# First loads reordered, the last softmax inverses spread by TensorE, and the last attention group written in separate steps

## The chip, the cores and the metric

The kernel runs on one core of a Trainium2 chip. The metric is the device time of one execution in microseconds (us). The engines are TensorE (PE, matrix products into PSUM), VectorE (DVE), ScalarE (ACT), GpSimd (POOL) and SyncE (SP, which only issues transfers here). Each works through its own instructions in order. Transfers (DMA) are issued from the queues of SP, ACT and POOL.

## The reference

One decoder block over 512 positions of width 1024 with two attention branches of 8 heads of 64 each, both fed by one input projection. Cut to what matters:

```python
h = rms_norm(x, norm_g)
fq, fk, fv, fz, mq, mk, mv, mz, ga, gb, fl = split_cols(h @ w_in, ...)
# FoX: causal softmax(q k^T / 8 + c_i - c_j), c the running sum of log_sigmoid(fl + b_f)
y_fox = fox_attention(norm(fq), norm(fk), fv, log_f) * silu(fz)
# MoBA: rope on q and k; own block causal, other blocks of 256 by top-k (all of them at this length)
y_moba = moba_attention(rope(norm(mq)), rope(norm(mk)), mv) * silu(mz)
merged = sigmoid(ga + b0) * (y_fox @ w_fox) + sigmoid(gb + b1) * (y_moba @ w_moba)
out = x + merged @ w_out
```

All is float32.

## The kernel before

**Products.** Each float32 operand is split into a high and a low part in the type float32r (`...h` and `...l`: the high one is a cast, mostly by ACT, the low one a subtraction by DVE). A product is three PE matmuls: high by high, high by low and low by high. `Zh`, `Zl` are the parts of the scaled input (one block of 128 channels by 512 positions for each `xt` of 256 KB), `wh_...`, `wl_...` those of the weights, which come in as `wr_...`.

**Start.** Eight matmuls on zeros (`warm_ps`, L82) precede the real ones. The constants `cs` (128x68, 35 KB, with the norm gains that `Zh` is scaled by) are loaded by the ACT queue. Then `load_g` loads a block xt and splits it, and `load_quarters` loads the first weights `wr_fqa` in pieces: the first k block by the ACT queue behind `cs`, the second by the SP queue behind xt0, each with a DVE cast of 128x256 of its own, and then two blocks at a time. Calls of both alternate, so the SP queue carries xt0, w1, xt1, xt2, w2:4, xt3, xt4, w4:6, xt5, xt6, w6:8, xt7. PE's first products (L358 to L360, `fqa`) use them.

**Attention.** Four groups of four heads follow: FoX a, FoX b, MoBA a, MoBA b. The functions of a group are `Tr(pr)` (transposes of the normed q and k of a pair of heads, L494 and L496, their scaling into `QS`, `KH`, and a transfer by the ACT queue that copies `KH` to the other 64 partitions, L507), `Aa(h)` (logits `lg` by L530 and L531, row maximum and mask by DVE, exponential by ACT with the row sum), `Bb(h)` (transposes of the probabilities, L576, into `p_a`, `p_b`, `p_cc`; their split into `pth` and `ptl`, L582 and L583; the products with v into `pv`, L586 and L587; the sum of both halves into `ypair` with the help of the copy `ysh`) and `Yp(pr)` (product with the inverse row sums and with silu(z), L626 and L627, and the split into `yh` and `yl`, called `yhm`, `ylm` in the MoBA branch).

**The inverse row sums.** `inverse_sums` takes the reciprocals, a 128x8 block with one column for a head and query tile. `sums_out` transposes it (`p_ri`, L555), copies it by ACT (`rinv_t`, L557) and stores it to DRAM; `sums_in` loads it back by two broadcast transfers of the ACT queue (L566) into `rinv_bc`, 64 partitions for each head. `Yp` multiplies by it.

**What stands between.** While a group is worked through, `inter` mixes its steps evenly with units of other products: the projections of the next group, and in the last group two units of `mzb` (`pz`) and six of `wf0` to `wf2` (`pf`, the FoX branch times its output weights, 12 matmuls of 128x512 a unit, L644 to L646). `wf3` follows the last group on its own.

**Gates.** Then come the gate projections `GA0`, `GA1`, `GB0`, `GB1`. Each is a Winograd scheme of seven products (`A11`, `S3`, `A12`, `S2`, `S1`, `A22`, `S4`; L715 to L718 into `pb_GA`), whose left sides are `Gh`, `Gl` or the sums `S0` to `S3`, which POOL's queue loads from DRAM (L258, eight loads). ACT copies some products out of PSUM (`e_GA`, L725) and splits the weights (`wh_GA`, L110); DVE makes `wl_GA` (L112). `Yp(1)` of the last group is emitted behind the third unit of `GA0`. Then come `wm0` to `wm3`, which use `yhm`, and the output products `wo0` to `wo3`.

**Order.** The program is written in this order; a scheduler then orders the instructions of each engine by its own simulated times, so an instruction can come earlier or later than it is written. All three change spots are subject to it.

Of the kernel before, what the change touches and what calls it, by code (L numbers as in the profile page):

```python
# [13 lines left out]
P = 128  # L14
# [15 lines left out]
def fox_moba_kernel(ctx: ExitStack, tc, xT, x, w_in, w_fl, w_fox, w_moba, w_out, cst, rope, out):  # L30
# [31 lines left out]

    cs = con.tile([P, C_END], F32, name="cs")
    rp = con.tile([P, NT, 32], F32, name="rp")
    wfl = con.tile([P, KT, 8], F32, name="wfl")
    nc.scalar.dma_start(out=cs, in_=cst)

# [6 lines left out]
    mask = con.tile([P, 512], F32, name="mask")  # L74
    wsc = t2("u", 4, "wsc", (P, 2))
# [18 lines left out]
    XT, Z = {}, {}  # L94

    def load_g(*ks):
        for k in ks:
            xt = XT[k] = t2("y", 15, f"xt{k}")
            nc.sync.dma_start(out=xt, in_=xT[:, k, :])
# [24 lines left out]
    def load_quarters(name, c0, hf, between):  # L124
        raw = sb.tile([P, 4, CW], F32, name=f"wr_{name}{hf}", tag="wr", bufs=WR)
        hi = sb.tile([P, 4, 264], F32R, name=f"wh_{name}{hf}", tag="wh", bufs=4)
        lo = sb.tile([P, 4, 264], F32R, name=f"wl_{name}{hf}", tag="wl", bufs=4)
        for q in range(2):
            first = hf == 0 and q == 0
            for k in (slice(0, 1), slice(1, 2)) if first else (slice(2 * q, 2 * q + 2),):  # L130
                (nc.scalar if first and k.start == 0 else nc.sync).dma_start(
                    out=raw[:, k], in_=w_in[c0 // CW, :, 4 * hf + k.start:4 * hf + k.stop, :])
                if first:
                    V.tensor_copy(hi[:, k, :CW], raw[:, k])
                else:
                    A.activation(hi[:, k, :CW], raw[:, k], AF.Copy)
                V.tensor_tensor(out=lo[:, k, :CW], in0=raw[:, k], in1=hi[:, k, :CW].bitcast(F32), op=OP.subtract)
            load_g(*between[q])
        chunks.setdefault(name, []).append((hi, lo))
# [343 lines left out]
    def attn_group(br, half, gq, gk):  # L483
# [76 lines left out]
        def sums_in(pr):  # L560
            if last and pr:
                rb = st["r", pr] = t2("u", 4, "rinv_bc")
            else:
                rb = st["r", pr] = stage["pool"].tile([P, S], F32, name="rinv_bc", tag="rinv_bc", bufs=1)
# [4 lines left out]
        def Bb(h):  # L569
            def go():  # L570
                pts, vt = st[h], VT[f"{br}v{half}"]
                o = h % 2
                pv = pst("pv", 1, "pv")
# [39 lines left out]
                if o == 0:  # L613
                    sums_out(pr)
                elif pr:
                    sums_in(1)
# [391 lines left out]
```

## Time and profile before

| | |
|---|---|
| three runs | 444.06, 443.63, 441.45 us; median 443.63 |
| profiled execution | 444.28 us, of which the span of the profile is 442.5 |
| mean granted PE clock | 0.996 |
| busy: PE, DVE, ACT, POOL | 428.4, 314.7, 262.5, 87.6 us |
| share of the span | 97%, 71%, 59%, 20% |
| read from and written to HBM | 46.27 and 6.32 MB |

Times in the rows count from the start of the span. A row of the timeline gives start, duration, engine, line, operation, result and operands, and in brackets the idle time before it with what ended it. A row of the waits gives the total, the count and the longest. The chain is the work that ended last, followed backwards; PEclk is the granted PE clock in tenths. Matmuls overlap, so the time of one is longer than the distance between two.

### The profile page before, as it was taken

What the parts mean: (1) busy time and instruction counts of PE and PEld (TensorE: products, weight loads), DVE (VectorE), ACT (ScalarE), POOL (GpSimd) and SP (SyncE); (2) the same over time, 40 slices, a digit from 0 to 9 for tenths busy, and PEclk for the clock granted to TensorE, in tenths of its full rate; (3) what the DMA queues carried; (4) which work ended last, traced back from release to release, by engine and by line L of the source; (5) the groups of instructions that cost most, each with busy time, mean ns of one, the idle gap of its engine ahead of it and who ended that gap; (6) DMA issues with size and microseconds to landing.
All of it is one profiled execution on the core that took longest, in us unless ns stands there. A gap on an engine that the chain in (4) does not pass through costs nothing.

```text
span 442.5 us, 8082 instructions
## 1 busy us (share of the span) xinstructions
PE 428.4 (97%) x3100; PEld 403.9 (91%) x3100; DVE 314.7 (71%) x563; ACT 262.5 (59%) x491; POOL 87.6 (20%) x106
## 2 busy tenths in 40 slices
PE   6999999999999999999999999987999999999996
PEld 5998899999999998899998878877999989989996
DVE  5559994777998869676956689928978786584311
ACT  5676544876777769887765876717655545531100
POOL 1059200224142950134621002200000000000000
PEclk9999999999999999999999999998999999999999
DMA  8962164424377413303304212663134405624231
GB/s 261 388 246 69 54 205 137 111 74 136 110 233 209 103 55 120 119 13 122 106 14 132 95 24 90 232 203 96 60 133 126 160 1 183 197 96 152 88 96 48
DMA packets 25991, 56.40 MB, mean 127 GB/s; under 512 B 3296, under 2 KB 11936, under 8 KB 25952
## 3 DMA queue, kind: packets, MB, share of 16 engines
q1 hardware_dynamic: 14528, 39.95, 27.4%
q10 hardware_dynamic: 10272, 11.74, 9.0%
q0 software_dynamic: 1152, 4.19, 2.8%
q8 instruction: 24, 0.39, 0.4%
q14 instruction: 15, 0.12, 0.1%
HBM read 46.27 MB, written 6.32 MB: 119 GB/s over the span
## 4 chain that ended last, share of the span: by engine, by line
PE 85%; ACT 6%; DMA 4%; DVE 2%; issue 1%; ACTq 0%; SPq 0%; DVEq 0%
PE pb_GB L718 3%; PE pb_GB L717 3%; PE pb_GB L715 3%; PE po L815 3%; PE po L817 3%; PE po L816 3%; PE pb_GA L715 2%; PE pb_GA L717 2%; PE pb_GA L718 2%; PE pv L587 2%; PE pv L586 2%; PE lg L530 2%; PE lg L531 2%; PE pm L644 2%; PE pm L645 2%; PE pm L646 2%
## 5 line engine op out<-in xcount | busy, mean ns | idle before, releaser
L535 ACT ACTIVATE p<-p,negm 128x128 f32<-128x128 f32 (+1 forms) x64 | 35.7, 558 | 12.5 <-DVE negm L533 11.2
L310 POOL TENSOR_TENSOR ff<-ss,mh 128x8 f32<-128x8 f32 x16 | 27.1, 1699 | 79.6 <-DVE ss L308 77.3
L533 DVE CUSTOM_DVE_ANT_0 p<-lg,mask 128x128 f32<-128x128 f32 (+1 forms) x64 | 30.5, 485 | 5.8 <-PE lg L531 5.6
L815 PE MATMUL po<-wh_wo,mgh 128*128 128x256 f32 x96 | 27.1, 282 | 0.0
L817 PE MATMUL po<-wh_wo,mgl 128*128 128x256 f32 x96 | 27.0, 282 | 0.0
L816 PE MATMUL po<-wl_wo,mgh 128*128 128x256 f32 x96 | 26.9, 281 | 0.0
L825 DVE TENSOR_TENSOR ot<-po,xr 128x256 f32<-128x256 f32 x16 | 6.6, 424 | 24.7 <-PE po L817 23.6
L110 ACT ACTIVATE wh_wo<-wr_wo 128x1024 fp32r<-128x1024 f32 x8 | 8.5, 1061 | 21.6 <-PE po L817 8.0
L530 PE MATMUL lg<-KH,QS 128*128 128x128 f32 (+1 forms) x64 | 20.7, 332 | 0.4 <-DMA KH<-KH 0.4
L112 DVE TENSOR_TENSOR wl_GB<-wr_gb,wh_GB 128x1024 fp32r<-128x1024 f32 x14 | 16.8, 1223 | 4.2 <-ACT wh_GB L110 3.3
L110 ACT ACTIVATE wh_GB<-wr_gb 128x1024 fp32r<-128x1024 f32 x14 | 14.6, 1059 | 8.6 <-PE pm L645 2.5
L612 DVE TENSOR_TENSOR ypair<-pv,ysh 64x512 f32<-64x512 f32 x16 | 11.0, 688 | 10.8 <-ACT ysh L611 10.7
L816 PEld LDWEIGHTS po<-wl_wo,mgh 128*128 128x128 f32 x96 | 18.1, 189 | 0.0
L815 PEld LDWEIGHTS po<-wh_wo,mgh 128*128 128x128 f32 x96 | 18.1, 189 | 0.0
L817 PEld LDWEIGHTS po<-wh_wo,mgl 128*128 128x128 f32 x96 | 18.1, 188 | 0.0
L715 PE MATMUL pb_GA<-Gh,wh_GA 128*128 128x256 f32 x48 | 14.3, 298 | 3.3 <-ACT e_GA L725 3.3
L112 DVE TENSOR_TENSOR wl_GA<-wr_ga,wh_GA 128x1024 fp32r<-128x1024 f32 x14 | 16.6, 1219 | 1.2 <-ACT wh_GA L110 1.1
L110 ACT ACTIVATE wh_GA<-wr_ga 128x1024 fp32r<-128x1024 f32 x14 | 14.5, 1054 | 4.5 <-DVE wr_ga L679 2.7
L504 DVE SCALAR_TENSOR_TENSOR QS<-p_qT,cs,QS 64x512 fp32r<-64x512 f32 x16 | 12.0, 750 | 6.6 <-ACT QS L503 6.2
L611 ACT ACTIVATE ysh<-pv 64x512 f32<-64x512 f32 x16 | 9.5, 593 | 9.8 <-PE pv L587 8.0
L112 DVE TENSOR_TENSOR wl_wo<-wr_wo,wh_wo 128x1024 fp32r<-128x1024 f32 x8 | 9.8, 1222 | 7.4 <-ACT wh_wo L110 7.4
L583 DVE TENSOR_TENSOR ptl<-p_a,pth 128x512 fp32r<-128x512 f32 x16 | 11.0, 687 | 5.1 <-ACT pth L582 5.0
(448 smaller groups left out, 1798.8 us busy)
## 6 DMA issues: line engine op xcount, KB each, us to landing
wr_ga<-in_w_in_dram SPq DMA_DIRECT2D x8, 512.0 KB
wr_gb<-in_w_in_dram SPq DMA_DIRECT2D x8, 512.0 KB
wr_wo<-in_w_out_dram SPq DMA_DIRECT2D x8, 512.0 KB
xt<-in_xT_dram SPq DMA_DIRECT2D x8, 256.0 KB
x<-in_x_dram SPq DMA_DIRECT2D x8, 256.0 KB
s_dramh<-sum_sh ACTq DMA_DIRECT2D x8, 256.0 KB
s_draml<-sum_sl ACTq DMA_DIRECT2D x8, 256.0 KB
KH<-KH ACTq DMA_DIRECT2D x16, 128.0 KB
```

What stands on the lines that cost most here:

```text
L110: A.activation(hi[:, :, 0:n], src, AF.Copy)
L112: eng.tensor_tensor(out=lo[:, q, 0:n], in0=src[:, q], in1=hi[:, q, 0:n].bitcast(F32), op=OP.subtract)
L310: G.tensor_tensor(out=f2, in0=ss.rearrange("p t h -> p (t h)"), in1=mh, op=OP.pow)
L530: T.matmul(lg[:, :n], qs[:, qt], kh[:, :n], start=True, stop=False)
L533: V.tensor_tensor_reduce(pt, lg[:, :n], mask[:, 512 - n:512], -0.125, 3.0e38, op0=OP.add, op1=OP.min, accum_out=mkn[:, hh, i:i + 1])
L535: A.activation(pt, pt, AF.Exp, bias=mkn[:, hh, i:i + 1], scale=-1.0, accum_out=rs[:, hh, i:i + 1])
L715: T.matmul(o, hi[:, k, cc], lh, start=(n < 3 and c == 0 and k == 0), stop=False, skip_group_check=True)
L717: T.matmul(o, hi[:, k, cc], ll, start=False, stop=False, skip_group_check=True)
L718: T.matmul(o, lo[:, k, cc], lh, start=False, stop=(k == 3), skip_group_check=True)
L815: T.matmul(p[:, :CW], gh[:, st], hi[:, k, :CW], start=(kk == 0), stop=False)
L816: T.matmul(p[:, :CW], gh[:, st], lo[:, k, :CW], start=False, stop=False)
L817: T.matmul(p[:, :CW], gl[:, st], hi[:, k, :CW], start=False, stop=(kk == KT - 1))
```

## The change

Three parts, all in the order or the way of work; what is computed stays the same.

1. **First loads.** `first_loads` issues all x blocks and first weights before anything else: xt0 and then `cs` by the ACT queue; w0:2 (256 KB in one), xt1, w2:4, xt2, xt3, w4:8 (512 KB in one), xt4 to xt7 by the SP queue. `first_split` makes one DVE cast of 128x512 for w0:2.
2. **The last pair's inverse sums.** For the last pair of heads of the last group `sums_out` and `sums_in` go. In `Yp(1)` POOL spreads the inverses into `rinv_w` (two copies of 128x4x64, an inverse repeated 64 times for each head and tile), four PE transposes put them into a PSUM bank (`p_rinv`, in place of a bank of `lg`), and DVE multiplies silu(z) by that bank.
3. **The last group.** `Bb(h)` becomes `Bb(h, 0)` (transposes and split) and `Bb(h, 1)` (products with v) for the heads 2 and 3, and the units of `mzb`, `wf0` to `wf3` stand at places written out by hand: after the steps 0, 2 and 5 one, after step 3 two, and one after each step from `Aa(3)` on, so one stands between the transposes of a head and its products. `wf3` is thus no longer behind the group.

```diff
--- before.py
+++ after.py
@@ -60,11 +60,33 @@
         return pst("tp", 3, name)
 
 
+    XT, RAW = {}, {}
+
+    def first_loads():
+        def xt(eng, k):
+            XT[k] = t2("y", 15, f"xt{k}")
+            eng.dma_start(out=XT[k], in_=xT[:, k, :])
+
+        def w(k0, k1):
+            hf = k0 // 4
+            if hf not in RAW:
+                RAW[hf] = sb.tile([P, 4, CW], F32, name=f"wr_fqa{hf}", tag="wr", bufs=WR)
+            nc.sync.dma_start(out=RAW[hf][:, k0 - 4 * hf:k1 - 4 * hf], in_=w_in[0, :, k0:k1, :])
+        xt(nc.scalar, 0)
+        w(0, 2)
+        nc.scalar.dma_start(out=cs, in_=cst)
+        xt(nc.sync, 1)
+        w(2, 4)
+        xt(nc.sync, 2)
+        xt(nc.sync, 3)
+        w(4, 8)
+        for k in range(4, KT):
+            xt(nc.sync, k)
+
+
     cs = con.tile([P, C_END], F32, name="cs")
     rp = con.tile([P, NT, 32], F32, name="rp")
     wfl = con.tile([P, KT, 8], F32, name="wfl")
-    nc.scalar.dma_start(out=cs, in_=cst)
-
     def col(c, n=1):
         return cs[:, c:c + n]
 
@@ -72,6 +94,8 @@
     triU = con.tile([P, P], F32, name="triU")
     ones = con.tile([P, P], F32, name="ones")
     mask = con.tile([P, 512], F32, name="mask")
+    enter("start")
+    first_loads()
     wsc = t2("u", 4, "wsc", (P, 2))
     V.memset(wsc, 0.0)
     A.activation(wsc, wsc, AF.Square)
@@ -91,12 +115,11 @@
 
     Gh = con.tile([P, KT, S], F32R, name="Gh")
     Gl = con.tile([P, KT, S], F32R, name="Gl")
-    XT, Z = {}, {}
-
-    def load_g(*ks):
+    Z = {}
+
+    def split_x(*ks):
         for k in ks:
-            xt = XT[k] = t2("y", 15, f"xt{k}")
-            nc.sync.dma_start(out=xt, in_=xT[:, k, :])
+            xt = XT[k]
             zh, zl = Z[k] = [stage["pool"].tile([P, S], F32R, name=f"Z{hl}{k}") for hl in "hl"]
             A.activation(zh, xt, AF.Copy, scale=col(C_NG + k))
             V.scalar_tensor_tensor(zl, xt, col(C_NG + k), zh.bitcast(F32), op0=OP.mult, op1=OP.subtract)
@@ -121,22 +144,19 @@
         V.tensor_tensor(out=lo[:, :, CW:264], in0=f, in1=hi[:, :, CW:264].bitcast(F32), op=OP.subtract)
         chunks.setdefault(name, []).append((hi, lo))
 
-    def load_quarters(name, c0, hf, between):
-        raw = sb.tile([P, 4, CW], F32, name=f"wr_{name}{hf}", tag="wr", bufs=WR)
-        hi = sb.tile([P, 4, 264], F32R, name=f"wh_{name}{hf}", tag="wh", bufs=4)
-        lo = sb.tile([P, 4, 264], F32R, name=f"wl_{name}{hf}", tag="wl", bufs=4)
+    def first_split(hf, between):
+        raw = RAW[hf]
+        hi = sb.tile([P, 4, 264], F32R, name=f"wh_fqa{hf}", tag="wh", bufs=4)
+        lo = sb.tile([P, 4, 264], F32R, name=f"wl_fqa{hf}", tag="wl", bufs=4)
         for q in range(2):
-            first = hf == 0 and q == 0
-            for k in (slice(0, 1), slice(1, 2)) if first else (slice(2 * q, 2 * q + 2),):
-                (nc.scalar if first and k.start == 0 else nc.sync).dma_start(
-                    out=raw[:, k], in_=w_in[c0 // CW, :, 4 * hf + k.start:4 * hf + k.stop, :])
-                if first:
-                    V.tensor_copy(hi[:, k, :CW], raw[:, k])
-                else:
-                    A.activation(hi[:, k, :CW], raw[:, k], AF.Copy)
-                V.tensor_tensor(out=lo[:, k, :CW], in0=raw[:, k], in1=hi[:, k, :CW].bitcast(F32), op=OP.subtract)
-            load_g(*between[q])
-        chunks.setdefault(name, []).append((hi, lo))
+            k = slice(2 * q, 2 * q + 2)
+            if hf == 0 and q == 0:
+                V.tensor_copy(hi[:, k, :CW], raw[:, k])
+            else:
+                A.activation(hi[:, k, :CW], raw[:, k], AF.Copy)
+            V.tensor_tensor(out=lo[:, k, :CW], in0=raw[:, k], in1=hi[:, k, :CW].bitcast(F32), op=OP.subtract)
+            split_x(*between[q])
+        chunks.setdefault("fqa", []).append((hi, lo))
 
     COLS = {}
     off = 0
@@ -559,18 +579,15 @@
 
         def sums_in(pr):
             if last and pr:
-                rb = st["r", pr] = t2("u", 4, "rinv_bc")
-            else:
-                rb = st["r", pr] = stage["pool"].tile([P, S], F32, name="rinv_bc", tag="rinv_bc", bufs=1)
+                return
+            rb = st["r", pr] = stage["pool"].tile([P, S], F32, name="rinv_bc", tag="rinv_bc", bufs=1)
             for o in range(2):
                 A.dma_start(out=rb[o * HD:(o + 1) * HD, :],
                             in_=R_dram[hb + 2 * pr + o].rearrange("t p -> (t p)").partition_broadcast(HD))
 
-        def Bb(h):
-            def go():
-                pts, vt = st[h], VT[f"{br}v{half}"]
-                o = h % 2
-                pv = pst("pv", 1, "pv")
+        def Bb(h, part=None):
+            def turn():
+                pts = st[h]
 
                 def blk(dst, i, j):
                     T.transpose(dst, pts[i][:, j * P:(j + 1) * P], ident)
@@ -582,9 +599,6 @@
                     A.activation(hi[:, :n], p[:, :n], AF.Copy)
                     V.tensor_tensor(out=lo[:, :n], in0=p[:, :n], in1=hi[:, :n].bitcast(F32), op=OP.subtract)
                     return hi, lo
-                def pvm(j, hl, c0, n, start, stop):
-                    T.matmul(pv[:, P * j:P * j + n], vt[:, j, h, :], hl[0][:, c0:c0 + n], start=start, stop=False)
-                    T.matmul(pv[:, P * j:P * j + n], vt[:, j, h, :], hl[1][:, c0:c0 + n], start=False, stop=stop)
                 pa = tp("p_a")
                 for i in range(4):
                     blk(pa[:, i * P:(i + 1) * P], i, 0)
@@ -598,6 +612,21 @@
                 for i in range(2, 4):
                     blk(pc[:, (i - 2) * P:(i - 1) * P], i, 2)
                 hc = spl(pc, 256)
+                st["t", h] = ha, hbb, hc
+
+            def go():
+                if part != 1:
+                    turn()
+                if part == 0:
+                    return
+                vt = VT[f"{br}v{half}"]
+                o = h % 2
+                ha, hbb, hc = st["t", h]
+                pv = pst("pv", 1, "pv")
+
+                def pvm(j, hl, c0, n, start, stop):
+                    T.matmul(pv[:, P * j:P * j + n], vt[:, j, h, :], hl[0][:, c0:c0 + n], start=start, stop=False)
+                    T.matmul(pv[:, P * j:P * j + n], vt[:, j, h, :], hl[1][:, c0:c0 + n], start=False, stop=stop)
                 pvm(0, ha, 0, 512, True, False)
                 pvm(1, hbb, 0, 384, False, False)
                 pvm(3, hbb, 384, 128, False, False)
@@ -610,7 +639,7 @@
                 sh = t2("u", 4, "ysh")
                 A.activation(sh[me, :], pv[ot, :], AF.Copy)
                 V.tensor_tensor(out=y[me, :], in0=pv[me, :], in1=sh[me, :], op=OP.add)
-                if o == 0:
+                if o == 0 and not (last and pr):
                     sums_out(pr)
                 elif pr:
                     sums_in(1)
@@ -622,8 +651,19 @@
                 gp = 2 * (half == "b") + pr
                 yh = t2("y", 15, f"yh{br}{gp}", dt=F32R)
                 yl = t2("y", 15, f"yl{br}{gp}", dt=F32R)
-                zr = st["r", pr]
-                (V if (br, gp) == ("m", 3) else G).tensor_tensor(out=zr, in0=ZS[br, gp], in1=zr, op=OP.mult)
+                if last and pr:
+                    zr, rb = ZS[br, gp], pst("lg", 2, "p_rinv")
+                    h0 = hb + 2 * pr
+                    rw = t2("u", 4, "rinv_w")
+                    for o in range(2):
+                        G.tensor_copy(rw.rearrange("p (t o d) -> p t o d", o=2, d=HD)[:, :, o, :],
+                                      ri[:, h0 + o, :, None].to_broadcast([P, NT, HD]))
+                    for t in range(NT):
+                        T.transpose(rb[:, t * P:(t + 1) * P], rw[:, t * P:(t + 1) * P], ident)
+                    V.tensor_tensor(out=zr, in0=zr, in1=rb, op=OP.mult)
+                else:
+                    zr = st["r", pr]
+                    G.tensor_tensor(out=zr, in0=ZS[br, gp], in1=zr, op=OP.mult)
                 V.tensor_tensor(out=y, in0=y, in1=zr, op=OP.mult)
                 A.activation(yh, y, AF.Copy)
                 V.tensor_tensor(out=yl, in0=y, in1=yh.bitcast(F32), op=OP.subtract)
@@ -631,7 +671,7 @@
             return go
 
 
-        return ([Tr(0)], [Aa(0), Aa(1), Tr(1), Bb(0), Aa(2), Bb(1), Yp(0), Aa(3)], [Bb(2), Bb(3)], [Yp(1)])
+        return ([Tr(0)], [Aa(0), Aa(1), Tr(1), Bb(0), Aa(2), Bb(1), Yp(0), Aa(3)], [Bb(2), Bb(3)] if not last else [Bb(2, 0), Bb(2, 1), Bb(3, 0), Bb(3, 1)], [Yp(1)])
 
 
     FS, MG = {}, {}
@@ -871,10 +911,9 @@
         for u in filler(names):
             u()
 
-    enter("start")
-    load_g(0)
-    load_quarters("fqa", COLS["fqa"], 0, ((1, 2), (3, 4)))
-    load_quarters("fqa", COLS["fqa"], 1, ((5, 6), (7,)))
+    split_x(0)
+    first_split(0, ((1, 2), (3, 4)))
+    first_split(1, ((5, 6), (7,)))
     nc.sync.dma_start(out=wfl, in_=w_fl)
     load_fl("fka", COLS["fka"], 0)
     load_fl("fka", COLS["fka"], 1)
@@ -926,11 +965,19 @@
                     u()
                     store[0]()
                 fill[2 * k + 8], fill[2 * k + 8 + 1] = with_sums, with_store
-        inter(body + ([following] if n < 3 else []) + tail, fill)
+        if n < 3:
+            inter(body + [following] + tail, fill)
+        else:
+            fill += filler(["wf3"])
+
+            for k, u in enumerate(body + tail):
+                u()
+                for f in {0: (0,), 2: (1,), 3: (2, 3), 5: (4,)}.get(k, (k - 3,) if k > 7 else ()):
+                    fill[f]()
+
         if n < 3:
             body, tail = nxt[1][:1] + gate + nxt[1][1:], nxt[2]
             gate = nxt[3]
-    seq(["wf3"])
     enter("gates")
     load_sums()
     fill = filler(["GA0", "GA1", "GB0"])
```

## The prediction

> **What bounds the kernel now.** I read the page's busy times and its slices first, then PE's waits, then the chain that ended last around the longest wait, and last the timeline of the first 8 us.
>
> ```profile
> span 442.5 us, 8082 instructions
> PE 428.4 (97%) x3100; PEld 403.9 (91%) x3100; DVE 314.7 (71%) x563; ACT 262.5 (59%) x491; POOL 87.6 (20%) x106
> PE   6999999999999999999999999987999999999996
> PEclk9999999999999999999999999998999999999999
> ```
>
> TensorE (PE) is busy for 97% of the span, so apart from PE's own work only 442.5 - 428.4 = 14.1 us of idle time can be won, and whatever PE does at a low clock. The slices show where: the first, a soft spot at slices 27 to 28, and the end. The sum below is made against this execution's own time of 444.28 us (span 442.5, and 1.8 around it). The median of the three runs is 443.63, the lowest 441.45. PE's waits, as total, times and longest:
>
> ```profile
> PE pb_GA L715 <- ACT e_GA L725: 3.3, 1, 3.3
> PE fqa L358 <- DVE wh_fqa L134: 2.4, 1, 2.4
> PE pv L586 <- ACT pth L582: 1.3, 2, 0.7
> PE pv L587 <- DVE ptl L583: 0.9, 1, 0.9
> PE lg L530 <- DMA KH<-KH: 0.4, 1, 0.4
> ```
>
> One wait of 3.34 us and one of 2.41 us stand out. The chain ahead of the first (start, duration, what; the row of `yhm` is the timeline's, the last a window's):
>
> ```profile
> 289.16 0.45 ACTq L566
> 289.65 6.68 DMA rinv_bc<-r_dram
> 296.42 0.70 DVE rinv_bc L626
> 297.88 0.63 ACT L628 ACTIVATE yhm<-ypair 128x512 fp32r<-128x512 f32 x1 [6.96 <-DVE ypair L627]
> 298.41 1.99 ACT wh_GA L110 x2
> 300.40 0.49 ACT e_GA L725
> 300.93 0.58 PE pb_GA L715
> 304.31 0.12 PE pb_GA L715
> 300.50:303.90 3.40, 2.97 (x14) 2.97 (x15) 3.37 (x4) 3.10 (x4) 0.00 (x0) 0.50 0.46 136
> ```
>
> The reciprocal sums of the last pair of heads go out to DRAM and come back broadcast (6.68 us for the way back alone). Two multiplications on VectorE (DVE, 0.70 each) need them, then `yhm` on ScalarE (ACT), which stood idle 6.96 us for it. Nobody needs `yhm` yet, but ACT works in order: two weight splits (`wh_GA`) and the copy `e_GA`, which PE needs to reuse a bank, stand behind it. So PE waits for a transfer whose result it does not use here. The last row (us, then busy time by engine, clock, DMA) shows what follows: a granted clock of 0.50 from 300.5 to 303.9, and 14 matmuls in 2.97 us, 0.21 each, instead of 0.12.
>
> The start of the kernel:
>
> ```profile
> 0.80 0.42 ACTq L66 DMA_DIRECT2D cs<-in_cst_dram  x1
> 0.81 0.38 SPq L99 DMA_DIRECT2D xt<-in_xT_dram  x1
> 1.24 0.41 SPq L131 DMA_DIRECT2D wr_fqa<-in_w_in_dram  x1
> 1.32 0.38 ACTq L131 DMA_DIRECT2D wr_fqa<-in_w_in_dram  x1
> 4.27 0.72 ACT L101 ACTIVATE Zh<-xt,cs 128x512 fp32r<-128x512 f32 x1 [1.52 <-DMA cs<-in_cst_dram]
> 5.97 0.29 DVE L134 CAST wh_fqa<-wr_fqa 128x256 fp32r<-128x256 f32 x1 [4.46 <-DMA wr_fqa<-in_w_in_dram]
> 6.64 0.74 DVE L102 SCALAR_TENSOR_TENSOR Zl<-xt,cs,Zh 128x512 fp32r<-128x512 f32 x1
> 7.31 0.28 DVE L134 CAST wh_fqa<-wr_fqa 128x256 fp32r<-128x256 f32 x1
> 7.74 1.19 PE L358 MATMUL fqa<-wh_fqa,Zh 128*128 128x256 f32 x4 [2.41 <-DVE wh_fqa L134]
> 13.20 0.79 PE fqa L358 x4
> 14.22 0.12 PE fqa L359
> ```
>
> The first matmul at 7.74 waits for the second cast of `wr_fqa` (7.31); that one stands on DVE behind others: the first cast, its remainder and `Zl` of block 0 come before it. The first cast itself waited until 5.97 for the second transfer of a queue. From 7.74 on PE takes 0.21 us a matmul, from about 13.8 on 0.12.
>
> **The change, part by part.**
>
> *First loads.* The bytes stay the same. The ACT queue now carries xt0 (256 KB) and then `cs`; the SP queue both quarters of the first weights in one transfer, then xt1 and the rest, with later x blocks behind later weights. DVE makes one cast of 128x512 where it made two of 128x256, and the changed order on DVE puts this cast ahead of the remainder and `Zl`. So PE needs: `cs` and xt0, then `Zh` (0.72 us), and the cast. Transfers in first place on a queue had landed by 4.27 (`cs` there, xt0 too, since `Zh` needs both); the ones in second place by 5.97. The weights are now first: they land near 4.3, plus 0.3 that I allow for the doubled first piece, and the cast takes 0.6 (twice 0.29), so they are ready near 5.2. `cs` is now second on its queue: between 4.27 and 5.97. The start of PE is thus between 4.27 + 0.72 = 5.0 and 5.97 + 0.72 = 6.7. A second-place transfer had 128 KB in those rows and `cs` is far smaller, so I take `cs` at 5.1 and the start at 5.9: 1.85 us earlier, between 0 (it also can wait for something that I do not see) and 2.7. What hides it later: nothing, if data keep up. PE's list of waits has none in this stretch after 7.74, and a lead of 1.85 is small against the loads of 512 KB that follow.
>
> The clock decides what these 1.85 us are worth. If the fast pace still begins at 13.8, the additional matmuls run at 0.21, and the gain is 1.85 x 0.12/0.21 = 1.06. If it begins as much earlier as PE does, it is 1.85. If it comes one window of 3.4 us earlier (the length of the slow stretch above), 1.06 + 3.4 x (1 - 0.12/0.21) = 2.5. I take the middle one, **-1.85**. The Trainium skill, "TensorE: Matmul & The Clock Gate", section "What's actually happening", says that the windows run freely, about 3.4 us each, and that one busy window releases the throttle. The slow stretch of 3.4 us agrees with it; counted back from 303.9 in such steps the trace's phase would give the last of these three values, and on the mean over phases the middle one.
>
> *The last pair's sums.* Removed: one transpose into `p_ri`, one ACT copy, one store, two broadcast loads. Added: two GpSimd (POOL) copies, four PE transposes, and DVE's product reads PSUM. The four transposes cost what four of the same shape cost:
>
> ```profile
> 267.07 0.44 PE p_a L576 x4
> 271.25 1.60 POOL L626 TENSOR_TENSOR rinv_bc<-zs_mzb,rinv_bc 128x512 f32<-128x512 f32 x1 [28.40 <-DMA rinv_bc<-r_dram]
> 30.56 0.25 POOL L333 TENSOR_TENSOR tab_mk<-rp,cs 128x32 f32<-128x32 f32 x1
> 286.86 0.54 POOL L258 DMA_DIRECT2D S3l<-s_draml  x1
> ```
>
> 0.44 + 0.1 for their start, less 0.1 for the lost transpose: **+0.45**. No row shows POOL copying 128x4x64 from a broadcast operand. By the rows it is between 0.25 (128x32) and 1.60 (128x512, two inputs); 128x256 elements are nearest to half the latter, so 0.8 each. POOL's queue holds the eight S loads ahead of these copies, the last of which is issued at 286.86. PE comes to the transposes only 67 matmuls of 0.12 after the last product with v, so 8 us cover the copies; were the cover gone, PE would wait at most 2 x 1.6 = 3.2 us. The two multiplications and `yhm` come later in the order of DVE and ACT, behind the weight splits and `e_GA`; what needs `yhm`, the products of `wm0`, comes after the whole of GA0, GA1 and GB0.
>
> So `e_GA` runs when its data are there, well ahead of PE's need, and the 3.34 us go: **-3.34**. Bounds: if another wait takes the place, for instance the weight splits which ran from 298.41 to 300.40 only because ACT was blocked, at most half comes back. With the gap goes the slow stretch: 14 matmuls took 2.97 us where 14 x 0.12 = 1.7 would do: **-1.3**, and 0 at the least. By the page just named an idle window throttles, and a gap of 3.34 us fills one of 3.4 us only in some phases; the runs at 441.45 and 443.63 may have escaped it. That changes what the change is worth against them, not the time after it.
>
> *The last group in steps.* The transposes of a head and its products with v are separate now, with units of the fox branch (`pf`, 12 matmuls each) put by hand between them, and the fourth unit group is among these instead of behind. PE's work is the same. Of PE's waits listed above, the shorter one for `pth` (1.3 - 0.7 = 0.6), that for `ptl` (0.9) and that for `KH` (0.4) are in this group: 1.9. Those for `pth` and `ptl` are a product following its own transposes; with 12 `pf` matmuls of 0.23 between, or 24 of the gate products of 0.12 behind the last head (2.8 us either way), most of them go. But what moves closer together can wait instead. ACT is the narrow one there:
>
> ```profile
> 250.00:260.00 10.00, 10.00 (x54) 8.42 (x53) 8.04 (x16) 9.83 (x18) 0.00 (x0) 1.00 0.08 19
> 280.08 0.23 PE pf L644
> 253.40 0.48 ACTq L507 DMA_DIRECT2D KH<-KH  x1
> 257.40 0.39 PE L530 MATMUL lg<-KH,QS 128*128 128x128 f32 x2
> ```
>
> ACT is busy 9.83 of these 10 us; `pf` matmuls take 0.23 us each (a row of the chain). In the changed order 12 `pf` matmuls stand between the transposes into `p_kT` and the first logits `lg` of the second pair, instead of 24: 12 x 0.23 = 2.8 us less cover. Those transposes come earlier than before, and the copy across partitions of `KH`, issued at 253.40 and needed at 257.40, moves with them. I count on new waits of 0.95 there (for a bank or for `KH`), 0.75 at the next `pth` and 0.6 at a bank that an ACT copy empties: 2.3, less the 1.9 that go: **+0.4**, between -1.9 (none is new) and +3 (each as long as `KH`'s below would allow).
>
> Sum: -1.85 + 0.45 - 3.34 - 1.3 + 0.4 = -5.64, so 444.28 - 5.64 = **438.6 us**.
>
> **Rivals.**
> 1. *The start does not move.* `cs` behind xt0 lands as late as the second-place transfers did (5.97), the first remainders come later, and data arrive no sooner. For it: the queues are shared out among all transfers in flight. The Trainium skill, "DMA: Bandwidth & Descriptors", section "Issuing engines are not separate DMA queues", speaks for this rival: another queue saves issue time only. Against it: the row of 5.97 shows that DVE's order, not only data, cost the time from 5.97 to 7.31. Time: 438.6 + 1.85 = 440.5.
> 2. *The waits move into the last group*: ACT being full, the new waits reach the upper bound of +3. Time: 438.6 + 2.6 = 441.2.
> 3. *The idle gap stays in part*: half the 3.34 us, with the slow stretch, because the weight splits are late by themselves. Against it: they followed `yhm` without a gap. Time: 438.6 + 1.7 + 1.3 = 441.6.
> 4. *Slower than before: `KH`'s copy lands behind PE.* The chain of the whole span shows one such copy on the path (first row; the others are the timeline):
>
> ```profile
> 117.41 4.70 DMA KH<-KH
> ...
> 180.16 1.28 ACT L535 ACT_TABLE_LOAD   x1
> 180.88 1.13 ACTq L566 DMA_DIRECT2D rinv_bc<-r_dram  x2
> ```
>
> My walk through the changed order with the durations above has PE at the logits at 252.0. If the copy is issued only when ACT has done the table load and the exponentials ahead of it (252.8), and takes those 4.70, it lands at 257.5, PE stands for 5.5 us and then loses 1.3 to the slow clock. Time: 438.6 - 0.95 + 5.5 + 1.3 = 444.5. It is slower than the median of before when the copy lands after 256.6 (444.5 - 443.63 = 0.9 earlier). Against it: a transfer of ACT's queue is issued while ACT loads a table, and does not wait for its end (here at 180.88, before the load of 180.16 is over), so the copy should land near 252.7.
> 5. *More than forecast*: the start at 5.0, no new waits: 444.28 - 2.7 + 0.45 - 3.34 - 1.3 - 1.9 = 435.5.
>
> **How the numbers follow.** A measurement of this kernel can tell about 1% from no change: faster means below 439.2, slower above 448.1. Chances: the forecast (436.5 to 440) 0.50, of which 0.42 lie below 439.2; the start not moving 0.13; waits in the last group 0.13; the gap in part 0.07; `KH` late 0.06; more than forecast 0.11. Faster: 0.42 + 0.11 + 0.02 of the first rival (where the clock helps) = 0.55. Slower: 0.04, from the fourth, where both heads of the pair wait, and from a mishap that I have not named. Same: 0.41. For the range I go from 434.5, past the fifth, to 443.5, past the first three; `KH` late and the tails stay out.
>
> **What would show it.** Right: PE's first `fqa` matmul between 5.0 and 6.7; no wait of PE for `pb_GA` behind `e_GA`; the granted clock at full in slice 27 to 28; four transposes into `p_rinv` within 0.6 us; PE's waits between 245 and 285 of 1 to 3 us in all; PE's busy time near 428.4 - 1.0 = 427. Wrong: a first matmul after 7.3; a wait for `KH` or `lg` of over 3 us near 252; a new wait behind `wl_GA` near 295; a lower clock in another place.

## The result

Eleven runs of each kernel: 441.06 us median for the changed kernel, 444.27 for the one before, a ratio of 0.9919 with an interval of 0.9895 to 0.9943. In a second comparison (the first experiment) it was 441.27 against 443.53, 0.9946 (0.9922 to 0.997). The change makes the kernel 2.3 to 3.2 us faster, about half of the 5.6 us forecast: both intervals lie below 1, but the gain is less than the 1% that the prediction called measurable. One of the eleven executions of the changed kernel, the one profiled, took 697.99 us at a clock of 0.56 from end to end; it is left out of the ratio, and the profile below is of the first experiment, 440.67 us with a span of 439.0.

Its page, busy times and the slices of PE's clock:

```profile
span 439.0 us, 8083 instructions
PE 427.2 (97%) x3103; PEld 402.8 (92%) x3103; DVE 315.6 (72%) x561; ACT 262.6 (60%) x490; POOL 89.0 (20%) x108
PEclk9999999999999999999999989999999999999999
```

PE's longest waits (total, times, longest), without the one ahead of the warm-up:

```profile
PE fqa L378 <- ACT Zh L124: 2.8, 1, 2.8
PE lg L550 <- DMA KH<-KH: 1.8, 2, 1.2
PE pv L628 <- ACT pth L599: 1.1, 2, 0.9
PE pf L684 <- DVE zs_mzb L418: 0.4, 1, 0.4
```

The wait of 3.3 for `pb_GA` is gone. The one at the start is longer than before (2.83 against 2.41), those for `KH` have grown from 0.4 to 1.8, and the soft spot of the clock is not gone but has moved: from slice 28 to slice 24, which is near 255 us. Of the 1.8, 0.6 stand near 122 us, in the second group, where the kernel before has its 0.4; 1.24 are new and in the last group. The start, in the timeline:

```profile
1.26 0.45 ACTq L77 DMA_DIRECT2D cs<-in_cst_dram  x1
5.42 0.43 DVE L154 CAST wh_fqa<-wr_fqa 128x512 fp32r<-128x512 f32 x1 [3.90 <-DMA wr_fqa<-in_w_in_dram]
7.40 1.34 ACT L124 ACTIVATE Zh<-xt,cs 128x512 fp32r<-128x512 f32 x2 [4.17 <-DMA cs<-in_cst_dram]
8.17 0.39 PE L378 MATMUL fqa<-wh_fqa,Zh 128*128 128x256 f32 x1 [2.83 <-ACT Zh L124]
```

The weights were there at 5.4, but `cs`, second on ACT's queue behind xt0, came at 7.4 (ACT idle 4.17 us until then). PE starts at 8.17 instead of 7.74. And the gate stage, in the timeline:

```profile
289.77 1.75 POOL L659 COPY rinv_w<-rinv 128x256 f32<-128x256 f32 x2
297.78 0.60 PE L662 MATMUL p_rinv<-ident,rinv_w 128*128 128x128 f32 x4
299.90 0.58 ACT L765 ACTIVATE e_GA<-pb_GA 128x512 f32<-128x512 f32 x1
300.38 0.62 ACT L668 ACTIVATE yhm<-ypair 128x512 fp32r<-128x512 f32 x1
```

The two POOL copies take 1.75 us in all and begin 8 us before PE's transposes; the four transposes start 0.36 us ahead of PE's next matmul; `yhm` runs after `e_GA`, and nobody waits.

For a table by stage I take from the timelines the starts of four instructions: the first `fqa` matmul, the first `fka` matmul, the first transpose of the last group's q, and the first output product `po`. The last column is the difference of the last two, the stretch of the last group, the gates and the merge.

| kernel | first fqa | first fka | last group's q | first po | stretch |
|---|---|---|---|---|---|
| before | 7.74 | 21.86 | 219.62 | 384.66 | 165.04 |
| changed | 8.17 | 21.14 | 219.72 | 381.08 | 161.36 |
| loads alone | 8.23 | 21.77 | 220.81 | 386.24 | 165.43 |
| inverse alone | 7.62 | 20.36 | 218.80 | 377.81 | 159.01 |
| steps alone | 7.38 | 18.81 | 217.79 | 383.43 | 165.64 |
| loads undone | 7.80 | 21.89 | 220.23 | 381.56 | 161.33 |
| steps undone | 7.93 | 20.91 | 219.23 | 378.25 | 159.02 |
| cs ahead | 8.67 | 21.62 | 219.84 | 381.21 | 161.37 |
| xt0 on SP | 6.27 | 19.92 | 218.73 | 377.73 | 159.00 |
| unit ahead | 8.28 | 22.29 | 220.95 | 379.97 | 159.02 |
| two more warm | 6.09 | 19.03 | 217.35 | 376.39 | 159.04 |

Two readings of it carry what follows. With the inverses by TensorE the stretch takes one of two values and repeats within 0.1 us (159.00 to 159.04, and 161.33 to 161.37), so it tells the parts apart better than medians do; with the DRAM trip it repeats less well (165.04 and 165.43 with the same last group). The time from the first `fqa` to the first `fka` does not repeat: 14.12, 12.74, 11.43 and 14.09 for the same loads. It depends on the clock, and its 2.7 us are half of the range of the runs of the kernel before in the first experiment (441.11 to 446.61).

### The profile page after: what moved, and what is told of

It reads as the page before. It is cut to its first block, busy times and chain, and to the rows that moved or that the text cites. A ratio compares the mean times of both kernels' runs of the same rounds, so it can differ in the third digit from the quotient of the medians.

```text
span 696.2 us, 8083 instructions
## 1 busy us (share of the span) xinstructions
PE 687.7 (99%) x3103; PEld 602.2 (86%) x3103; DVE 316.6 (45%) x561; ACT 266.5 (38%) x490; POOL 82.2 (12%) x108
## 4 chain that ended last, share of the span: by engine, by line
PE 98%; DMA 1%; ACT 0%; ACTq 0%; DVE 0%; issue 0%
PE pb_GA L757 3%; PE pb_GA L755 3%; PE pb_GB L758 3%; PE pb_GB L757 3%; PE pb_GB L755 3%; PE pb_GA L758 3%; PE po L855 3%; PE po L857 3%; PE po L856 3%; PE lg L551 2%; PE pv L628 2%; PE pv L629 2%; PE lg L550 2%; PE pm L684 2%; PE pf L684 2%; PE pm L686 2%
## 5 line engine op out<-in xcount | busy, mean ns | idle before, releaser
L856 PE MATMUL po<-wl_wo,mgh 128*128 128x256 f32 x96 | 36.7, 383 | 0.0
L856 PEld LDWEIGHTS po<-wl_wo,mgh 128*128 128x128 f32 x96 | 28.2, 294 | 0.0
L855 PEld LDWEIGHTS po<-wh_wo,mgh 128*128 128x128 f32 x96 | 28.2, 294 | 0.0
L857 PEld LDWEIGHTS po<-wh_wo,mgl 128*128 128x128 f32 x96 | 28.1, 293 | 0.0
L684 PE MATMUL pf<-yhf,wh_wf 128*128 128x512 f32 x32 | 18.8, 587 | 0.0
L686 PE MATMUL pf<-yhf,wl_wf 128*128 128x512 f32 x32 | 18.7, 584 | 0.0
L684 PE MATMUL pm<-yhm,wh_wm 128*128 128x512 f32 x32 | 18.7, 583 | 0.0
L757 PE MATMUL pb_GB<-Gl,wh_GB 128*128 128x256 f32 x48 | 18.6, 387 | 0.0
L686 PE MATMUL pm<-yhm,wl_wm 128*128 128x512 f32 x32 | 18.4, 576 | 0.0
L755 PE MATMUL pb_GB<-Gh,wh_GB 128*128 128x256 f32 x48 | 18.4, 383 | 0.0
```

The costliest lines, as they stand in the source:

```text
L684: T.matmul(p, hi[:, k, cc], yh, start=(k == 0), stop=False)
L686: T.matmul(p, lo[:, k, cc], yh, start=False, stop=(k == 3))
L755: T.matmul(o, hi[:, k, cc], lh, start=(n < 3 and c == 0 and k == 0), stop=False, skip_group_check=True)
L757: T.matmul(o, hi[:, k, cc], ll, start=False, stop=False, skip_group_check=True)
L855: T.matmul(p[:, :CW], gh[:, st], hi[:, k, :CW], start=(kk == 0), stop=False)
L856: T.matmul(p[:, :CW], gh[:, st], lo[:, k, :CW], start=False, stop=False)
```

## The experiments

**The changed kernel again and each part alone.** The first was the kernel as changed.

> The changed kernel itself, for a profile at the full clock. The prediction's sum: first fqa matmul near 5.9 instead of 7.74 (-1.85), no wait of 3.34 for pb_GA and no slow stretch behind it (-4.6), four transposes (+0.45), waits of the last group 2.3 instead of 1.9 (+0.4): 5.6 us less than the profile of before. The measured medians are only 3.2 apart. Rival A (the start does not move): first matmul at 7.3 or later, the rest as predicted. Rival B (the waits move): waits of PE between 245 and 285 of 4 us or more. Rival C (the slow stretch is not a constant part of before): before of this run has no clock of 0.5 near 300, and the gain without it is 4.3.

440.67 us for the profiled execution; rival A holds (8.17). Rival C does not: the profile of the kernel before has the slow stretch, and so have those of the loads alone (from 303.17 on) and of the steps alone (from 299.48 on). The waits in the last group are below rival B's bound, but they brought a slow stretch that no rival but the fourth had. A window of 3.4 us with these waits and the one behind it (us, then busy time of PE, PEld, DVE, ACT, POOL with counts, clock, DMA share, GB/s):

```profile
251.60:255.00 3.40, 1.65 (x7) 0.91 (x6) 3.11 (x8) 3.34 (x8) 0.00 (x0) 1.00 0.18 39
255.00:258.40 3.40, 3.40 (x10) 2.61 (x9) 3.30 (x9) 3.35 (x5) 0.00 (x0) 0.50 0.18 39
```

The timeline of the same place:

```profile
250.74 0.48 ACTq L527 DMA_DIRECT2D KH<-KH  x1
253.12 0.30 PE L550 MATMUL lg<-KH,QS 128*128 128x128 f32 x1 [1.24 <-DMA KH<-KH]
253.68 0.49 PE L628 MATMUL pv<-pth,v_mvb 128*128 128x512 f32 x1 [0.16 <-ACT pth L599]
254.53 0.50 PE L684 MATMUL pf<-yhf,wh_wf 128*128 128x512 f32 x1 [0.35 <-DVE zs_mzb L418]
255.16 0.63 PE L686 MATMUL pf<-yhf,wl_wf 128*128 128x512 f32 x1
258.51 0.39 PE L685 MATMUL pf<-ylf,wh_wf 128*128 128x512 f32 x1
```

`KH`'s copy, issued at 250.74, is there just ahead of 253.1, 1.24 us after PE wanted it. PE is busy for 1.65 of 3.40 us, then the clock is 0.50 for 3.4 us: eight `pf` matmuls take from 255.16 to 258.51, 3.35 us where 8 x 0.23 = 1.84 would do, so 1.5 are lost. The three waits add up to 1.24 + 0.16 + 0.35 = 1.75.

The copy of `KH` is not all that PE stands for here. The same logits need one of two banks, which DVE reads until 252.9 (first row below, the timeline's), and the chain that ended last goes past the copy (the other rows):

```profile
252.37 0.54 DVE L553 CUSTOM_DVE_ANT_0 p<-lg,mask 128x384 f32<-128x384 f32 x1
250.92 0.75 DVE QS L524
251.70 0.75 DVE KL L528
253.18 0.52 DVE ylm L669
253.79 0.69 DVE zs_mzb L418
```

DVE makes `QS` and `KL` of `Tr(1)` first; `ylm` and the copy of `zs_mzb`, which empties the bank for the next `pf` matmul, come behind, and that matmul starts at 254.53. By these rows PE would have stood there even with `KH` in time. No run takes the copy away, so how the cost divides between it and the order on DVE is not shown.

The loads alone:

```diff
-    nc.scalar.dma_start(out=cs, in_=cst)
+    first_loads()   # and first_split for load_quarters, as in the diff above
```

> Only the first loads and the first split are changed. Prediction's step: 1.85 us faster, first matmul near 5.9. Rival (the start moves but the clock or the data give it back): first matmul near 5.9 and less than 1 us faster, since the fast pace begins at the same time or a later block of xt or weights is waited for. Rival (the start does not move): 0.

444.58 us against 443.53, ratio 1.0033 (1.0008 to 1.0058): slower, by 1.5 us (0.0033 x 443.5; 1.05 between the medians). The first matmul comes at 8.23. PE's two longest waits:

```profile
PE pb_GA L735 <- ACT e_GA L745: 3.5, 1, 3.5
PE fqa L378 <- ACT Zh L124: 2.9, 1, 2.9
```

What PE waits for there, in the timeline:

```profile
7.45 1.34 ACT L124 ACTIVATE Zh<-xt,cs 128x512 fp32r<-128x512 f32 x2 [4.23 <-DMA cs<-in_cst_dram]
```

`cs` is as late as in the changed kernel. The later start does not explain the loss by itself: the first `fka` matmul comes no later than before (21.77 against 21.86), and 1.3 us are lost between it and the last group's q, where the wait for `KH` near 122 us is 1.2 instead of 0.4.

The inverse alone:

```diff
-            if last and pr: rb = ... "rinv_bc"   # and the two broadcast loads
+            if last and pr: return               # and rinv_w, p_rinv in Yp
```

> Only the last pair's inverse sums go by TensorE. Prediction's step: the wait of 3.34 and the slow stretch go, the transposes cost 0.45: 4.2 us faster (2.9 without the clock's part). Rival (another wait takes its place): PE waits for wl_GA or e_GA at the same spot for 1 us or more, and the gain is under 2.

437.62 us against 443.53, ratio 0.9876 (0.9843 to 0.9909): this part by itself is worth more than the whole change. The span of the gate products, first to last `pb_GA`, in windows of both kernels (before, then inverse alone):

```profile
280.62:333.58 52.96, 48.65 (x388) 47.52 (x386) 39.38 (x44) 28.02 (x40) 1.61 (x3) 0.97 0.39 132
```

```profile
279.79:326.73 46.94, 46.91 (x390) 46.41 (x389) 39.64 (x44) 27.87 (x39) 3.35 (x5) 1.00 0.42 143
```

Its waits in PE's list that are left in the last group or ahead of it:

```profile
PE pv L585 <- ACT pth L581: 1.4, 2, 0.8
PE pf L654 <- DVE f L668: 0.4, 1, 0.4
```

52.96 - 48.65 = 4.31 us of PE idle became 0.03, and 48.65 us of busy time became 46.91 although four transposes were added. The first is the wait of 3.34 and that of 0.9 for `ptl`, which also went; the second the slow stretch (1.3) and, with the transposes set off, some 0.8. The starts of PE's matmuls place most of that: the first four products with v of the last head take 1.40 us (from 285.85 on) where they take 1.11 with the inverse alone, and at each of the two waits the next start is put off by 0.16 to 0.17 more than the idle time, since a matmul's time (0.28) is longer than the distance between two (0.12). In the last group 1.4 - 0.8 = 0.6 of the waits for `pth` is left, and 0.4 for `f`: 1.0.

The steps alone:

```diff
-        return (..., [Bb(2), Bb(3)], [Yp(1)])
+        return (..., [Bb(2), Bb(3)] if not last else [Bb(2, 0), Bb(2, 1), Bb(3, 0), Bb(3, 1)], [Yp(1)])
+        # and the units placed by hand, wf3 among them
```

> Only the last group's transposes and products with v are separate steps with the units between, the sums go through DRAM as before. Prediction's step: +0.4 (between -1.9 and +3). Since the DRAM trip is still there, and its end moves with the last product with v, the wait for pb_GA stays near 3.3 or grows where fewer gate products stand behind it. Rival: this part alone costs 2 us or more, which is where the missing 2.4 us of the prediction went.

444.41 us against 443.53, ratio 1.0021 (0.999 to 1.0052): nothing that can be told from none; the stretch is 0.6 longer. Two of its waits:

```profile
PE pb_GA L725 <- ACT e_GA L735: 2.9, 1, 2.9
PE lg L530 <- DMA KH<-KH: 2.1, 2, 1.3
```

And two windows in the last group:

```profile
248.28:251.69 3.41, 2.07 (x12) 1.34 (x10) 3.08 (x7) 3.38 (x6) 0.00 (x0) 1.00 0.27 75
251.69:255.10 3.41, 2.99 (x12) 2.25 (x13) 3.38 (x9) 3.33 (x7) 0.00 (x0) 1.00 0.18 38
```

The wait for `KH` is there as in the changed kernel (1.26 up to 251.20; the rest of the 2.1 is in the second group), and so is the one of 0.35 behind it. But in this execution no slow stretch follows. The clock of this trace changes at 5.93, 299.48 and 302.89, so 86 and 87 steps of 3.41 us after the first change; the windows above are laid out in these steps, and the two waits fall into different ones, with 2.07 and 2.99 us of busy time.

**One part undone at a time.** The loads:

> The changed kernel with the first loads as before: inverse by TensorE and the steps stay. Theory (new waits in the last group and the slow stretch that they bring cost what is missing): PE waits for KH and others near 252, about 1.8 us in all, with or without a slow stretch of 3.4 us behind them; the time is 440 to 441 (the loads alone cost 0 to 1). Rival (it is the loads that ate the gain): 437.6 as in the run with the inverse alone.

440.62 us against 444.04, ratio 0.9921 (0.9891 to 0.9951). The theory holds: with the old loads the stretch is 161.33 as in the changed kernel. The wait at the same place, and the windows of the wait and of the slow stretch, which is there again:

```profile
PE lg L530 <- ACT yhm L648: 1.3, 1, 1.3
```

```profile
252.73:256.14 3.41, 2.00 (x8) 1.41 (x9) 3.15 (x9) 3.36 (x8) 0.00 (x0) 1.00 0.08 17
256.14:259.55 3.41, 3.41 (x10) 2.63 (x9) 3.06 (x8) 3.35 (x5) 0.00 (x0) 0.50 0.18 38
```

The wait ends at 253.65. The list names `yhm`, which ends at that moment; the wait of 0.9 that it has for `KH` is in the second group. With the 0.35 of the next `pf` matmul the new waits are 1.6, not 1.8.

The steps undone:

> The changed kernel with the last group as before: loads reordered and the inverse by TensorE. Theory: no KH wait of over 0.5 us and no slow stretch near 255; the time is 438 to 439 (437.6 of the inverse alone plus 0 to 1 for the loads). Rival (loads): 441.

439.51 us, ratio 0.9903 (0.9869 to 0.9936); the stretch 159.02. The expected 438 to 439 was a little low; the median alone, against the changed kernel's ratios 0.9919 and 0.9946, tells little, the stretch does: 161.36 - 159.02 = 2.3 us of it hang on the third part. They are accounted for: waits of 1.75 in place of 1.0, and the 1.5 lost to the slow clock. (The one wait for `KH` in this run's list, 0.5, is in the second group.)

**Why cs was late.** The edit, in the changed kernel:

```diff
-        xt(nc.scalar, 0)
-        w(0, 2)
         nc.scalar.dma_start(out=cs, in_=cst)
+        xt(nc.scalar, 0)
+        w(0, 2)
```

> The changed kernel, but the ACT queue issues cs ahead of xt0. Theory A (the ACT queue as a whole had moved its 290 KB only by 7.4, being served less than SP's): cs lands by 4.5, xt0 near 7.4, first matmul near 8.1, time as the changed kernel. Theory B (only the small rows of cs came late): xt0 lands near 5.5, first matmul near 6.3, 1 to 2 us faster than the changed kernel.

Theory A. 441.05 us, ratio 0.9935 (0.9907 to 0.9962), no change to the changed kernel. `Zh` now waits for xt0, not for `cs`, and begins even later:

```profile
4.38 0.43 DVE L154 CAST wh_fqa<-wr_fqa 128x512 fp32r<-128x512 f32 x1 [2.86 <-DMA wr_fqa<-in_w_in_dram]
7.90 2.13 ACT L124 ACTIVATE Zh<-xt,cs 128x512 fp32r<-128x512 f32 x3 [0.34 <-DMA xt<-in_xT_dram]
8.67 0.39 PE L378 MATMUL fqa<-wh_fqa,Zh 128*128 128x256 f32 x1 [3.34 <-ACT Zh L124]
```

In either order the 290 KB on ACT's queue (xt0 and `cs`) were complete only between 7.4 and 7.9, while SP's queue delivered its first 256 KB by 4.4 or 5.4. The small rows of `cs` were not the cause; what is put second on the queue beside SP's long list is late.

So xt0 goes to the head of SP's queue:

```diff
-        xt(nc.scalar, 0)
-        w(0, 2)
         nc.scalar.dma_start(out=cs, in_=cst)
+        xt(nc.sync, 0)
+        w(0, 2)
```

> Loads: cs alone on the ACT queue, SP carries xt0, w0:2, xt1, w2:4 and the rest as in the changed kernel; inverse by TensorE; last group as before. By theory A of the run with cs ahead: cs and xt0 land by 4.5, w0:2 near 5.3, first matmul near 5.9, and 1 to 2 us faster than the run with the steps undone: about 437. Rival (the clock gives the earlier start back): first matmul near 5.9, but the first fka matmul no earlier than in the other runs, and no gain.

437.04 us, ratio 0.9841 (0.9804 to 0.9878), against 0.9903 for the steps undone, whose text differs by this alone (the intervals overlap by 0.0009). The timeline, then the windows around the start:

```profile
4.32 0.72 ACT L124 ACTIVATE Zh<-xt,cs 128x512 fp32r<-128x512 f32 x1 [1.56 <-DMA cs<-in_cst_dram]
5.69 0.43 DVE L154 CAST wh_fqa<-wr_fqa 128x512 fp32r<-128x512 f32 x1 [4.18 <-DMA wr_fqa<-in_w_in_dram]
6.27 0.71 PE L378 MATMUL fqa<-wh_fqa,Zh 128*128 128x256 f32 x4 [1.05 <-DVE wh_fqa L154]
7.44 0.39 PE L379 MATMUL fqa<-wl_fqa,Zh 128*128 128x256 f32 x1 [0.46 <-DVE wl_fqa L157]
```

```profile
5.10:8.50 3.40, 1.89 (x13) 1.60 (x13) 2.44 (x4) 1.13 (x2) 0.00 (x0) 0.98 0.96 340
8.50:11.90 3.40, 3.40 (x18) 3.40 (x18) 2.66 (x4) 2.83 (x6) 0.00 (x0) 0.52 1.04 380
```

`cs` and xt0 land by 4.3, the weights at 5.7, PE begins at 6.27. The forecast for the change, 5.9, was a fair one for this order of loads. Of the 1.66 us by which the start is earlier than with the steps undone, the first `fka` matmul keeps 1.0: the first `fqa` matmuls run at the full pace (four in 0.71), then PE idles 0.46 for `wl_fqa`, and from 8.4 on the clock is halved (0.52 in the window) for 3.4 us.

**The last group: which line costs it.** The scheduler decides the order, so steps that are written apart need not end up apart. The smallest difference in the text that could cost the 2.3 us is the place of one unit: the first of `wf0` is written behind `Tr(1)` in the changed kernel, and ahead of it before. The edit:

```diff
-                for f in {0: (0,), 2: (1,), 3: (2, 3), 5: (4,)}.get(k, ...):
+                for f in {0: (0,), 2: (1, 2), 3: (3,), 5: (4,)}.get(k, ...):
```

> The changed kernel with one unit placed elsewhere: the first unit of wf0 stands ahead of Tr(1) of the last group instead of behind it; the steps stay separate. Theory: PE's order in the last group is then that of the run with the steps undone, so the whole cost of the third part lies in this one place: no wait for KH of over 0.5 us, no slow stretch near 255, 159.0 us from the first transposes of mqb to the first output product instead of 161.4, and 438.5 to 439.5 in all. Rival (the separate steps themselves cost it): 161.4 in that stretch and 441 in all.

439.0 us against 444.24, ratio 0.9878 (0.9849 to 0.9906); the stretch is 159.02, and PE, DVE and ACT work through the same instructions in the same order as in the run with the steps undone. The same windows as in the changed kernel, then the issue of the first `KH` copy and two rows of DVE, then PE's one wait for `KH`:

```profile
251.60:255.00 3.40, 3.40 (x20) 2.87 (x18) 2.56 (x5) 3.39 (x9) 0.00 (x0) 1.00 0.06 23
255.00:258.40 3.40, 3.40 (x16) 2.76 (x15) 3.33 (x8) 3.30 (x4) 0.00 (x0) 1.00 0.18 39
```

```profile
254.74 0.48 ACTq L527 DMA_DIRECT2D KH<-KH  x1
254.20 0.68 DVE L418 COPY zs_mzb<-pz_mzb 128x512 f32<-128x512 f32 x1
255.39 0.74 DVE L524 SCALAR_TENSOR_TENSOR QS<-p_qT,cs,QS 64x512 fp32r<-64x512 f32 x1
```

```profile
123.47 0.30 PE L550 MATMUL lg<-KH,QS 128*128 128x128 f32 x1 [0.79 <-DMA KH<-KH]
```

PE is busy throughout, at the full clock. `Tr(1)` comes later here: its `KH` copy is issued at 254.74 instead of 250.74, DVE makes `QS` behind the copy of `zs_mzb` and not ahead of it, and with more `pf` matmuls ahead of its logits PE has work for the time. The one wait for `KH`, 0.8, is in the second group; the last group has none, as expected. So the separate steps by themselves leave no trace in this order, and the 2.3 us are the price of `Tr(1)` standing ahead of one unit of 12 matmuls.

**The idle time after the warm-up.** In the run with xt0 on SP:

```diff
-WARM = 8
+WARM = 10
```

> The run with xt0 on SP's queue, with ten warm-up matmuls instead of eight, so that PE is idle for 0 to 0.5 us ahead of its first real matmul instead of 0.94. Theory (the slow stretch of 3.4 us in the first products comes from the idle time after the warm-up): the products run 0.12 apart from the start on in most runs, the first fka matmul comes near 18.3 instead of 19.9, and the time is 1 to 1.6 us less: 435.5 to 436. Rival (the slow stretch comes whatever PE did ahead of it, or the first product waits for the warm-up): 437 or more.

436.04 us (435.84 to 437.11) against 444.24, ratio 0.982 (0.9792 to 0.9849), at the upper end of what was expected. The same windows as for eight:

```profile
5.10:8.50 3.40, 3.40 (x17) 2.50 (x16) 2.44 (x4) 0.83 (x3) 0.00 (x0) 1.00 1.02 333
8.50:11.90 3.40, 3.11 (x24) 2.71 (x24) 2.24 (x4) 2.79 (x5) 0.00 (x0) 1.00 1.03 394
```

The slow stretch is gone: 24 matmuls in the second window instead of 18. The pace is not 0.12 from the start on, as expected: the first four products take 1.20 us here and 0.71 with eight, and only from 7.2 on is the pace full. The first `fka` matmul comes at 19.03, 0.9 earlier than with eight and 0.7 later than I expected, since PE now waits for its operands (0.29 in that window). The median is 1.0 below that of eight, but the intervals overlap. Nor do the two profiles decide it: the clock first rises at 4.93 in one and at 7.16 in the other, so the windows lie differently too. The mean clocks of all executions point to the warm-up, 0.998 to 1.0 in all five with ten, but 0.995 or 0.996 in three of six with eight (a slow stretch of 3.4 us makes 0.004); that is few, and the gain of this step by itself is not shown. Against the kernel before, this version has the lowest ratio of all.

## Why the prediction was right or wrong

*The sum.* Forecast -5.6; by parts the runs give +1.5 for the loads alone (0.65 between the medians of the changed kernel and of the loads undone, which were taken on two chips), -5.9 for the inverse (443.53 to 437.62) and +2.3 for the last group, together -2.1 to -3.0; the change measured -2.3 and -3.2. The direction and the range held, the likeliest value did not: 441.06 against 438.6, and a time below 439.2, which had 0.55, did not come. That the range held is in part luck: the loads were off by 2.5 to 3.4 us and the last group by 1.9 one way, the inverse by 1.7 the other. The first two rivals, 440.5 and 441.2, came nearer, and something of both happened.

*First loads, -1.85: wrong in sign.* The step that failed is "I take `cs` at 5.1", and its bounds 4.27 to 5.97 with it. They were read from transfers in second place on a queue whose first transfer was small (35 KB); behind 256 KB the second place came at 7.4. The first rival had the place right ("lands as late as the second-place transfers did") and its price too low. The DVE part of the step was right: one cast ahead of the remainders does let PE start as soon as the data are there, as the run with xt0 on SP shows (6.27).

*The clock at the start* was treated as three cases with the middle one taken. The runs show that it is not one number: in the four profiles with the old loads the clock first rises near 13.8, 10.7, 5.9 and 13.8 us, and the first `fka` comes 11.4 to 14.1 us after the first `fqa`. Which one an execution gets depends on where its windows of 3.4 us lie, so a start that is 1.7 us earlier brought 1.0 in one pair of profiles. That agrees with the page of the Trainium skill cited in the prediction, "TensorE: Matmul & The Clock Gate", section "What's actually happening", which has free-running windows.

*The inverse sums, -3.34 - 1.3 + 0.45 = -4.2: right in mechanism, too small.* Measured -6.0 in the stretch. Both terms are seen, the transposes too (the next start is 0.36 later, against 0.44), and POOL's copies (1.75 in all against the 1.6 taken). The prediction thought that some runs escape the slow stretch, since the gap must fill a window; all three profiles with the DRAM trip have it, the kernel before with a window that was busy for 0.50 of 3.41 us ahead of it. What was missed is the wait of 0.9 for `ptl`, which I had put with the last group and which this part removed (the run of the steps alone still has it; how it went is not shown), and 0.8 of busy time.

*The last group, +0.4: mis-sized, +2.3.* The new waits were 1.75 where I had 2.3, the ones that they replace 1.0 where I had 1.9, so that difference was near (0.75 against 0.4). One of the 1.9 was misread: the wait of 0.4 for `KH` stands at 122 us, in the second group. The term left out is the slow stretch that waits of this length can bring: I booked it only in the fourth rival, for a wait of 5.5. And the reason given was wrong in one point: I took the 12 matmuls between transposes and products for the work of the separate steps. The lists show that the steps leave no trace; the one thing that counts is what the fourth rival and the cover of 12 instead of 24 `pf` matmuls were about, `Tr(1)` moved ahead. That rival's mechanism was at work at most on a smaller scale: the copy of `KH` was issued at 250.74, not 252.8, and took 2.3 us, not 4.7, so that PE waited 1.24, not 5.5; and by the rows the bank of these logits and the order on DVE would have held PE at the same place.

*What was named as a sign* came out so: no wait for `pb_GA`, transposes within 0.6, PE busy 427.2 against 427 forecast, new waits of 1.75 in the last group (1 to 3), first matmul later than 7.3 (the sign for wrong), the clock lower in another place (also for wrong).

## What to carry to other kernels

Where a transfer result is multiplied in by an engine that works in order, look at what stands behind that instruction: here a DRAM trip whose product nobody needed for a long time held up copies that PE needed, and replacing the trip was worth 6 us. Price a new wait of PE with the slow clock that may follow it, not by its length alone. And with a scheduler between text and engines, compare the instruction lists of the variants first: the separate steps did not reach the chip, and one unit's place did.

## What the runs showed of the hardware

I had not expected that a wait of about half a window can halve the clock. In every profile the clock changes at whole steps of 3.41 us from its first change, so the windows can be laid out. PE was busy for 1.65 of the 3.4 us ahead of the slow stretch in the changed kernel, for 2.00 of 3.41 in the run with the loads undone, and for 1.89 of 3.4 at the start with xt0 on SP, each followed by a stretch of 3.4 us at half the clock. In the run of the steps alone nearly the same waits fell into two windows, with 2.07 and 2.99 us busy, and no slow stretch followed; nor did one at its start, behind 1.97 of 3.42. So near half these busy times, whose ends are modelled, do not tell which way it goes, and the same waits can cost 1.5 us more or not, by where they fall. The page of the Trainium skill, "TensorE: Matmul & The Clock Gate", section "What's actually happening", has the throttle return after an idle window; in these rows half-busy ones did it, and the measurement decides.

Two queues were not served alike: with more than 1 MB asked for by SP's queue at the same time, 290 KB on ACT's took until 7.4 us in one order and 7.9 in the other, while the first place on SP's queue was there between 4.3 and 5.4. In the changed kernel SP's queue had moved 0.88 MB by 7.4 us, ACT's 0.30.
